# Statistics tiles of the closing rows with six entries instead of five, in a one-core encoder layer

## The chip, the cores and the metric

The kernel runs on one core of a Trainium2 chip. The core has five engines that run beside each other: TensorE (PE, matrix products; its loads of the stationary operand have rows of their own, PEld), VectorE (DVE), ScalarE (ACT), GpSimd (POOL) and SyncE (SP, which issues most of the transfers here). Sixteen transfer engines (DMA) move data between the device memory and the on-chip memory SBUF. SBUF has 128 partitions; a tile takes the same byte range in each of them, so "a tile begins at byte 38,784" means that byte of every partition. Products are summed up in PSUM, a second on-chip memory.

The metric is the device time of one launch in microseconds. The median of three runs is given, and beside it the time of the execution that was profiled.

## What is computed

One layer of an encoder for 256 positions and width 2,048, in float32: windowed attention with rotary positions and a sink, a squared-ReLU MLP with 8,192 hidden values, both with a scale, shift and gate that are worked out from a condition vector `c`, and a LayerNorm behind each.

```python
mod = c_act @ mod_w[i] + mod_b[i]
sh_m, sc_m, g_m, sh_f, sc_f, g_f = jnp.split(mod, 6, axis=-1)
hmix = x * (1.0 + sc_m[:, None, :]) + sh_m[:, None, :]
y = windowed_gqa_sink(hmix, positions, ...)
x = layer_norm(DEEPNORM_ALPHA * x + (1.0 + g_m[:, None, :]) * y, ln_mix_g[i], ln_mix_b[i])
hff = x * (1.0 + sc_f[:, None, :]) + sh_f[:, None, :]
y = sq_relu_mlp(hff, mlp_w1[i], mlp_b1[i], mlp_w2[i], mlp_b2[i])
x = layer_norm(DEEPNORM_ALPHA * x + (1.0 + g_f[:, None, :]) * y, ln_mlp_g[i], ln_mlp_b[i])
```

The last line is the one that the edited lines belong to: the closing LayerNorm, whose mean and variance are gathered in the statistics tiles.

## The kernel before

**Weights.** All weights are read once, in pieces of 1 MB: 128 partitions with 8 KB each, one row of 8 KB for each partition. `Stream.loads` (line 228) issues them on SyncE's queue, in the order of a list that is put together ahead of the loop, each as soon as one of the buffers named `raw` is free. Every product of the layer is made in three parts, from operands that are split into a rounded high half and a remainder: ScalarE rounds a half of a `raw` tile into a `wh` tile (line 298), VectorE subtracts it from the `raw` tile into a `wl` tile (line 249), and TensorE multiplies high by high, high by low and low by high. These three are lines 554, 555 and 556 (helper `mm3`), 1112 and 1114 in the MLP's first product, and 1082, 1085 and 1086 in its first block. For the condition's product, `raw` tiles are used as they are, by TensorE (line 362) or by VectorE (line 402).

**Stages.** First come the condition's columns and the query, key and value product, then attention and its output product, then the MLP in four blocks of 2,048 hidden values. In blocks 1 to 3, `ff_mixed` makes a part of the second product with seven instead of eight products of half size (Strassen's scheme): its left operands are tiles `u` (from the pool of tiles named `g4`, which the profile calls `g`) and their sums and differences in a tile `sc` (helper `sides`, lines 1054 to 1059). Its right operands lie in `wh`, `wl` and, for two of four, in a further `raw` tile. Of the seven products four take `sc` as the stationary operand and three take `u`.

**The closing rows.** Behind block 3, `add_gated` (lines 837, 838, 840) multiplies a piece of 128 x 512 by the gate, adds it to the residual and notes its statistics with `bn_stats`: six numbers for a piece, in `st[t]` for row tile t (0 or 1). Row tile 0 has four pieces. Row tile 1 has five, since its last piece is split in two. `norm_scalars` and `last_scalars` then aggregate the numbers (lines 844 and 1267), and the rows are scaled and stored to `out` with rows of 2 KB. There are two pairs of tiles called `st0` and `st1`: one for the LayerNorm behind attention (line 964, four entries) and one for the closing one (line 1247). They share their slots, two for each name, and a slot is as large as the larger of its tiles, rounded up to 32 bytes.

**Where tiles lie.** The pools are laid out one behind the other: constants (`cst`), small tiles (`sml`: `sc`, `mrow`, the attention's scalars, `st0` and `st1`, four tiles of 2 KB that many names share, and the LayerNorm's scalars), then `raw`, `wh`, `wl` and the twenty 4 KB tiles `g4`; last a stretch that holds three more `raw` tiles first and six 4 KB tiles `g4b` later. In the built program of before they begin at these bytes:

| tiles | first begins at | past a multiple of 2,048 |
| --- | --- | --- |
| `sc` (4 KB) | 20,480 | 0 |
| `mrow` (2 x 2 KB) | 24,576 | 0 |
| four shared tiles of 2 KB | 29,824 | 1,152 |
| `raw` (5 x 8 KB) | 38,784 | 1,920 |
| `wh` (5 x 4 KB) | 79,744 | 1,920 |
| `wl` (5 x 4 KB) | 100,224 | 1,920 |
| `g4` (20 x 4 KB) | 120,704 | 1,920 |
| `raw` (3 more), `g4b` (6 x 4 KB) | 202,624 | 1,920 |

The order of the instructions on each engine is set by a scheduler from the order of the code and from priorities (`AHEAD`), partly by hand (`STEPS`, `LOADS`); neither sees an address.

Of the kernel before, what the change touches and what calls it, by code (L numbers as in the profile page):

```python
# [11 lines left out]
F32 = mybir.dt.float32  # L12
# [9 lines left out]
NT = S // 128  # L22
# [38 lines left out]
def hybrid_kernel(ctx: ExitStack, tc: tile.TileContext, a, out: bass.AP):  # L61
    nc = tc.nc
    cst = ctx.enter_context(tc.tile_pool(name="cst", bufs=1))
    sml = ctx.enter_context(tc.tile_pool(name="sml", bufs=4))
# [485 lines left out]
    def part(tiles, t, c):  # L550
        return tiles[c][:, t * 512:t * 512 + 512]
# [282 lines left out]
    def add_gated(ps, t, c, gt, stats, cols=slice(0, 512), n=0):  # L834
        tmp = sml.tile([128, 512], F32, name="tmp", tag="t2", bufs=4)
        z = part(xs, t, c)[:, cols]
        nc.vector.tensor_tensor(tmp[:, cols], ps[:, cols], gt(c)[:, cols], op=OP.mult)
        nc.vector.tensor_add(z, z, tmp[:, cols])
        if stats:
            nc.vector.bn_stats(stats[t][:, c + n], z)  # L840

    def norm_scalars(st):
        mv = sml.tile([128, 2], F32, name="mv")
        nc.vector.bn_aggr(mv, st)
        ve = sml.tile([128, 1], F32, name="ve")
        nc.vector.tensor_scalar_add(ve, mv[:, 1:2], LN_EPS)
        sd = sml.tile([128, 1], F32, name="sd")
        nc.scalar.activation(sd, ve, AF.Sqrt)
        r0 = sml.tile([128, 1], F32, name="r0")
        nc.vector.reciprocal(r0, sd)  # L850
        q = sml.tile([128, 1], F32, name="qq")
        nc.vector.scalar_tensor_tensor(q, r0, ve, r0, op0=OP.mult, op1=OP.mult)
        nc.vector.tensor_scalar(q, q, -0.5, 1.5, op0=OP.mult, op1=OP.add)
        nc.vector.tensor_mul(r0, r0, q)
        return mv, r0
# [67 lines left out]
    for n in range(21):  # L923
# [37 lines left out]
        if n == 16:  # L961
            warm = sml.tile([128, 1], F32, name="warm")
            nc.scalar.activation(warm, eps, AF.Sqrt)
            st = [sml.tile([128, 4, 6], F32, name=f"st{t}", bufs=2) for t in range(NT)]
# [197 lines left out]
    def gather(pm):  # L1162

        y = [part(ys, t, c) for t in range(NT) for c in range(2)]
        w = sml.tile([128, 512], F32, name="w", tag="t2", bufs=4)

        def add(d, *ops):
            return lambda: nc.vector.tensor_add(d, *ops)

        return [add(y[0], y[0], pm[2]), lambda: nc.scalar.copy(w, pm[6]), add(y[1], y[1], pm[3]),  # L1170
                add(y[2], y[2], pm[4]), add(y[0], y[0], pm[1]), add(w, w, pm[1]), add(y[1], y[1], w),
                add(y[1], y[1], pm[5]), add(y[3], y[3], pm[5]), add(w, w, pm[7]), add(y[2], y[2], w),
                add(y[3], y[3], w)]
# [70 lines left out]
    for n in range(2):  # L1244
        for h in range(2):
            nc.gpsimd.dma_start(gb[n][h], a["lnrow"][2 + n:3 + n, h * 1024:h * 1024 + 1024].partition_broadcast(128))
    st = [sml.tile([128, 5, 6], F32, name=f"st{t}", bufs=2) for t in range(NT)]
    mid = gather(pm)
    for f in mid[:2]:
        f()  # L1250
# [13 lines left out]
    def last_scalars(st, g):  # L1264

        mv = sml.tile([128, 2], F32, name="mv")
        keep(nc.vector.bn_aggr(mv, st))
        dm = sml.tile([128, 128], F32, name="dm", tag="t2", bufs=4)
        keep(nc.vector.tensor_scalar(dm, ident, mv[:, 0:1], 0.5, op0=OP.mult, op1=OP.mult))
        sd = sml.tile([128, 1], F32, name="sd")  # L1270
        keep(nc.scalar.activation(sd, mv[:, 1:2], AF.Sqrt, bias=eps))
        ve = sml.tile([128, 1], F32, name="ve")
        keep(nc.vector.tensor_scalar_add(ve, mv[:, 1:2], LN_EPS))
        z = part(xs, 1, 3)
        keep(nc.vector.scalar_tensor_tensor(z, z, mv[:, 0:1], g, op0=OP.subtract, op1=OP.mult))
        r0 = sml.tile([128, 1], F32, name="r0")
        keep(nc.vector.reciprocal(r0, sd))
        q = sml.tile([128, 1], F32, name="qq")
        keep(nc.vector.scalar_tensor_tensor(q, r0, ve, r0, op0=OP.mult, op1=OP.mult))
        keep(nc.vector.scalar_tensor_tensor(q, q, -3.0, r0, op0=OP.add, op1=OP.mult))  # L1280
        return q, dm
# [16 lines left out]
    mv, rstd = norm_scalars(st[0][:, :4])  # L1298
# [7 lines left out]
    gneg = sml.tile([128, 512], F32, name="w", tag="t2", bufs=4)  # L1306
# [21 lines left out]
        keep(nc.tensor.matmul(pw[c], ident, part(xs, 1, c), start=True, stop=False))  # L1328
    with tc.high_priority(200):
        add_gated(pr, 1, 3, g2, st, right, 1)  # L1330
        rstd, dm = last_scalars(st[1], gneg)
    for c in (3, 1, 2, 0):
        z, (g, b) = part(xs, 1, c), affine(c)
        if c < 3:
# [96 lines left out]
```

## Time and profile before

| what | us |
| --- | --- |
| median of 3 runs | 1073.85 |
| lowest and highest | 1073.42 and 1074.5 |
| profiled execution | 1074.7 |
| its span, first to last instruction | 1072.9 |

How to read the rows that follow. A group's row gives the line, the engine, the operation, what is written and read, the shape, how many there are, and behind the bar the busy time in us and the mean of one in ns; behind the second bar stands the idle time of the engine ahead of them. A row by stretch gives for each engine the busy time and, in brackets, the instructions; then the granted clock of TensorE as a share, the mean busy share of the 16 transfer engines, and what they moved in GB/s. A row of a transfer queue gives packets, megabytes and the time that its packets took as a share of 16 engines over the stretch that was asked for. The chain is followed back from the last instruction, at each step to what released it.

The granted clock was 0.999 over the span. The loads of the activations, which are used for comparison below, are these (size of one, and us from issue to landing):

```profile
g<-in_xT SPq DMA_DIRECT2D x2, 512.0 KB, 11.2
...
out<-g SPq DMA_DIRECT2D x4, 256.0 KB, 2.4
out<-g ACTq DMA_DIRECT2D x4, 256.0 KB, 2.5
g<-in_xT SPq DMA_DIRECT2D x3, 256.0 KB, 13.8
```

### The profile page before, as it was taken

The numbers are of one execution on the slowest core, as the hardware profiler recorded it, in microseconds if no ns is written. First come the engines' busy times: TensorE is split into PE (matmuls) and PEld (weight loads), VectorE is DVE, ScalarE is ACT, GpSimd is POOL, SyncE is SP. The second block draws the span as 40 slices with busy tenths as digits, with TensorE's granted clock in tenths as the row PEclk, the third lists the DMA queues.
The fourth block names the chain that finished last, engine by engine and source line by source line (L and its number), as shares of the span: only waits on it lengthen the run. The fifth ranks groups of instructions, "written<-read, shape, count | busy, mean of one in ns | idle before, by whom it ended". The sixth has DMA issues, their size and how long they took to land.

```text
span 1072.9 us, 16023 instructions
## 1 busy us (share of the span) xinstructions
PE 1055.0 (98%) x6188; PEld 856.2 (80%) x6188; DVE 939.5 (88%) x1401; ACT 619.9 (58%) x977; POOL 27.5 (3%) x54
## 2 busy tenths in 40 slices
PE   8999999999999999999999999999999999999998
PEld 6677677667677799988888888788888888888886
DVE  4689999989899998987579899899889887999998
ACT  5433347777672637643367777347677546777740
POOL 1000000001000000000000000000000001000000
PEclk9999999999999999999999999999999999999999
DMA  9999998798965898698725645973554773465742
GB/s 379 419 419 419 421 421 312 278 385 337 379 262 205 333 359 301 263 330 326 284 84 192 235 168 179 375 298 134 219 220 153 289 287 127 181 235 188 257 184 78
DMA packets 43516, 292.72 MB, mean 273 GB/s; under 512 B 5152, under 2 KB 5280, under 8 KB 9648
## 3 DMA queue, kind: packets, MB, share of 16 engines
q1 hardware_dynamic: 39456, 279.85, 67.6%
q0 software_dynamic: 3232, 10.50, 2.9%
q10 hardware_dynamic: 752, 1.35, 0.4%
q8 instruction: 48, 0.79, 0.3%
q14 instruction: 28, 0.23, 0.1%
HBM read 289.57 MB, written 2.11 MB: 272 GB/s over the span
## 4 chain that ended last, share of the span: by engine, by line
PE 83%; DMA 8%; DVE 7%; ACT 1%; issue 1%; SPq 0%; DVEq 0%; ACTq 0%
PE pa L1112 16%; PE pa L554 13%; PE pa L556 13%; PE pa L555 13%; PE pa L1114 8%; DMA raw<-in_modm 4%; PE pa L1085 3%; PE pm L362 3%; PE pa L1086 3%; PE pa L1082 3%; DMA raw<-in_w 2%; DVE g L402 2%; DVE wl L249 1%; PE pa L767 1%; DMA raw<-in_wqkv 1%; DMA raw<-in_modf 1%
## 5 line engine op out<-in xcount | busy, mean ns | idle before, releaser
L298 ACT CAST wh<-raw 128x1024 fp32r<-128x1024 f32 (+1 forms) x332 | 336.2, 1021 | 277.5 <-PE pa L556 150.7
L249 DVE TENSOR_TENSOR wl<-raw,wh 128x1024 fp32r<-128x1024 f32 (+1 forms) x332 | 388.0, 1182 | 68.0 <-ACT wh L298 63.1
L554 PE MATMUL pa<-wh,g 128*128 128x512 f32 x648 | 258.3, 399 | 3.2 <-ACT g L577 2.5
L556 PE MATMUL pa<-wh,g 128*128 128x512 f32 x648 | 253.1, 392 | 2.2 <-DVE g L579 2.2
L555 PE MATMUL pa<-wl,g 128*128 128x512 f32 x648 | 253.3, 391 | 0.8 <-DVE wl L249 0.8
L1112 PE MATMUL pa<-g,wh 128*128 128x512 f32 x768 | 192.3, 392 | 0.0
L1112 PEld LDWEIGHTS pa<-g,wh 128*128 128x128 f32 x768 | 140.6, 188 | 29.1 <-issue 0.8
L554 PEld LDWEIGHTS pa<-wh,g 128*128 128x128 f32 x648 | 121.6, 188 | 40.9 <-issue 6.8
L556 PEld LDWEIGHTS pa<-wh,g 128*128 128x128 f32 x648 | 121.5, 188 | 31.1 <-DVE g L579 4.1
L555 PEld LDWEIGHTS pa<-wl,g 128*128 128x128 f32 x648 | 121.8, 188 | 25.8 <-DVE wl L249 1.3
L1114 PEld LDWEIGHTS pa<-g,wl 128*128 128x128 f32 x768 | 104.7, 190 | 7.6
L1114 PE MATMUL pa<-g,wl 128*128 128x256 f32 x768 | 107.0, 282 | 0.0
L402 DVE SCALAR_TENSOR_TENSOR g<-raw,cact,g 128x1024 f32<-128x1024 f32 x66 | 83.9, 1279 | 4.1 <-DMA raw<-in_modf 2.7
L1085 PE MATMUL pa<-g,wh 128*128 128x256 f32 x256 | 72.9, 285 | 0.3 <-DVE g L1008 0.2
L1082 PE MATMUL pa<-g,wh 128*128 128x256 f32 x256 | 72.7, 285 | 0.3 <-ACT g L1000 0.3
L1086 PE MATMUL pa<-g,wl 128*128 128x256 f32 x256 | 72.3, 283 | 0.0
L249 DVE TENSOR_TENSOR raw<-raw 128x1024 fp32r<-128x1024 f32 x48 | 58.4, 1221 | 0.6 <-ACT raw L298 0.6
L298 ACT CAST raw<-raw 128x1024 fp32r<-128x1024 f32 x48 | 49.8, 1043 | 2.9 <-DVE raw L260 1.6
L1085 PEld LDWEIGHTS pa<-g,wh 128*128 128x128 f32 x256 | 49.1, 192 | 1.4 <-DVE g L1008 0.9
L1082 PEld LDWEIGHTS pa<-g,wh 128*128 128x128 f32 x256 | 49.0, 192 | 0.8 <-ACT g L1000 0.8
L1086 PEld LDWEIGHTS pa<-g,wl 128*128 128x128 f32 x256 | 49.1, 192 | 0.0
L402 DVE SCALAR_TENSOR_TENSOR g4b<-raw,cact,g4b 128x1024 f32<-128x1024 f32 x32 | 40.1, 1280 | 10.1 <-DMA raw<-in_modgf 10.1
(234 smaller groups left out, 1256.1 us busy)
## 6 DMA issues: line engine op xcount, KB each, us to landing
raw<-in_w1b SPq DMA_DIRECT2D x48, 1024.0 KB, 6.5
raw<-in_w SPq DMA_DIRECT2D x40, 1024.0 KB, 7.2
raw<-in_modm SPq DMA_DIRECT2D x32, 1024.0 KB, 12.3
raw<-in_modf SPq DMA_DIRECT2D x32, 1024.0 KB, 7.3
raw<-in_wqkv SPq DMA_DIRECT2D x24, 1024.0 KB, 13.0
raw<-in_w2s SPq DMA_DIRECT2D x24, 1024.0 KB, 4.9
raw<-in_modgm SPq DMA_DIRECT2D x16, 1024.0 KB, 6.5
raw<-in_wo SPq DMA_DIRECT2D x16, 1024.0 KB, 7.0
```

Source lines behind the costliest of these rows:

```text
L249: self.pinned(nc.vector.tensor_sub(l[:, :w], r, f32(self.hs[n])[:, :w]))
L298: self.pinned(nc.scalar.copy(h[:, :s.shape[-1]], s))
L362: i = nc.tensor.matmul(self.ps[32 * j:32 * j + 32, :w], lhsT[j] if type(lhsT) is list else lhsT, rhs[j], start=self.first, stop=stop)
L402: nc.vector.scalar_tensor_tensor(p[:, :e], s, cact[:, kt:kt + 1], p[:, :e], op0=OP.mult, op1=OP.add)
L554: nc.tensor.matmul(ps, xh, wh, start=start, stop=False)
L555: nc.tensor.matmul(ps, xh, wl, start=False, stop=False)
L556: S.prev = nc.tensor.matmul(ps, xl, wh, start=False, stop=stop).ins
L1082: x = nc.tensor.matmul(o, wh(w, 128), hh, start=new, stop=False)
L1085: nc.tensor.matmul(o, wh(w, 128), hl, start=False, stop=False)
L1086: nc.tensor.matmul(o, wl(w, 128), hh, start=False, stop=end)
L1112: nc.tensor.matmul(ps, wh(k, 128), ff_in(k), start=k == 0, stop=False)
L1114: nc.tensor.matmul(ps[:, :256], wl(k, 128), ff_in(k)[:, :256], start=False, stop=k == NK - 1)
```

## The change

The closing statistics tiles get room for six entries instead of five. The one aggregate that took the whole tile takes its first five entries.

```diff
-    st = [sml.tile([128, 5, 6], F32, name=f"st{t}", bufs=2) for t in range(NT)]
+    st = [sml.tile([128, 6, 6], F32, name=f"st{t}", bufs=2) for t in range(NT)]
...
-        rstd, dm = last_scalars(st[1], gneg)
+        rstd, dm = last_scalars(st[1][:, :5], gneg)
```

A tile of before has 5 x 6 x 4 = 120 bytes for each partition and a slot of 128; now it has 144 bytes and a slot of 160. With four slots, all that lies behind them is moved by 4 x 32 = 128 bytes:

| tiles | begin at, before | now | past a multiple of 2,048, now |
| --- | --- | --- | --- |
| `sc`, `mrow` | 20,480; 24,576 | the same | 0 |
| four shared tiles of 2 KB | 29,824 | 29,952 | 1,280 |
| `raw` | 38,784 | 38,912 | 0 |
| `wh` | 79,744 | 79,872 | 0 |
| `wl` | 100,224 | 100,352 | 0 |
| `g4` | 120,704 | 120,832 | 0 |
| `raw` (3 more), `g4b` | 202,624 | 202,752 | 0 |

The instructions of all engines stand in the same order as before, with the same operands by name, the same buffers and the same waits.

## The prediction

> **What bounds the kernel now.** I read the page first: shares, then the 40 slices, then the chain that ended last.
>
> ```profile
> span 1072.9 us, 16023 instructions
> ...
> PE 1055.0 (98%) x6188; PEld 856.2 (80%) x6188; DVE 939.5 (88%) x1401; ACT 619.9 (58%) x977; POOL 27.5 (3%) x54
> ...
> GB/s 379 419 419 419 421 421 312 278 385 337 379 262 205 333 359 301 263 330 326 284 84 192 235 168 179 375 298 134 219 220 153 289 287 127 181 235 188 257 184 78
> ...
> PE 83%; DMA 8%; DVE 7%; ACT 1%; issue 1%; SPq 0%; DVEq 0%; ACTq 0%
> ```
>
> TensorE is busy 98% of the span and carries 83% of the chain; transfers carry 8%, which is 86 us. The rate row shows that the transfers are not spread evenly: from the second slice to the sixth it stands still at 419 to 421 GB/s, and it never does so again. So there are two regimes, and I asked for busy time by stretch around their border, and for the chain of the first 170 us.
>
> ```profile
> core 0: us, PE busy (x) PEld busy (x) DVE busy (x) ACT busy (x) POOL busy (x), PEclk, DMA share, GB/s
> 27.00:134.00 107.00, 101.05 (x892) 74.59 (x891) 88.33 (x130) 36.87 (x50) 1.91 (x2) 1.00 1.01 419
> 134.00:161.00 27.00, 27.00 (x132) 19.59 (x131) 25.80 (x35) 12.17 (x16) 0.00 (x0) 1.00 1.01 420
> ```
>
> Up to 134 us the 16 transfer engines are full (share 1.01) while TensorE has 107 - 101.05 = 5.95 us of idle time: the loads set the pace there, and what they gain TensorE can use, up to 5.95 us. From 134 to 161 us it has none, though the engines are still full: it works off what has come, and a lead gained by 134 us is kept. Later, transfers matter only where the chain names them.
>
> ```profile
> by line: DMA raw<-in_modm 24.3%; PE pa L554 15.4%; PE pa L556 15.0%; PE pa L555 14.4%; PE pm L362 10.6%; DMA raw<-in_wqkv 6.6%; DVE g L402 2.2%; issue 1.9%; PE pa L177 1.6%; PE pt L745 1.0%; SPq L228 1.0%; PE pa L664 0.8%; PE pa L767 0.7%;
> ...
> 2.58 11.97 DMA raw<-in_modm
> ```
>
> Of the chain's 86 us of transfers, (24.3% + 6.6%) x 170 = 53 us lie in these first 170 us, and 33 us are scattered behind them. The loads begin at 2.6 us, so the stretch that they pace is 134 - 2.6 = 131 us long.
>
> **The change part by part.** No instruction is added, removed or moved on any engine, and no wait changes. Only addresses do: four small tiles take 32 bytes more each, so everything that is allocated behind them begins 128 bytes later. That includes every buffer that a load fills, and nearly every operand. Before, those tiles begin 1,920 bytes past a multiple of 2,048 (so half-way between two multiples of 256), afterwards on one. The distances between them stay as they are. So the sum has no term for a step of the program; it has a term for each way in which an address could set a duration.
>
> The statistics themselves: the same 9 writes of 6 numbers each go into rows of 36 numbers instead of 30, and the two aggregates still read 24 and 30 numbers that lie side by side. I take 0 for these.
>
> *Term 1, loads into the moved buffers.* Every load of before writes SBUF at such a half-way address, so the trace holds no load on the other kind. It is bounded by what a row pays beyond its bytes. A saturated 8 KB row takes 1.01 x 16 engines x 8,192 B / 419 GB/s = 316 ns. For 2 KB rows I use a stretch in which the loads of xT pass, then the closing stores, which read such addresses and write `out`.
>
> ```profile
> DMA packets 111, 0.30 MB, mean 396 GB/s; under 512 B 14, under 2 KB 14, under 8 KB 95
> ...
> q1 hardware_dynamic: 111, 0.30, 100.7%
> ```
>
> ```profile
> DMA packets 304, 0.56 MB, mean 371 GB/s; under 512 B 32, under 2 KB 32, under 8 KB 304
> ...
> q10 hardware_dynamic: 229, 0.44, 78.7%
> q1 hardware_dynamic: 75, 0.12, 22.3%
> ```
>
> The first is 62.00 to 62.75 us: 14 completions, 81 rows of 2 KB and 16 of 8 KB took 1.007 x 16 x 750 = 12,084 ns. Without 16 x 316 and 14 x 9.75 (from the next row) 6,891 ns are left, 85.1 ns a row. The second is 1,061.0 to 1,062.5 us: (1.01 x 16 x 1,500 - 32 x 9.75) / 272 = 88.0 ns a row. A load, which writes off a 256-byte line in SBUF, is not dearer than a store, which does not write there. From 85.1 and 316 ns a byte costs (316 - 85.1) / 6,144 = 0.0376 ns, and what a row pays beyond its bytes is 85.1 - 77.0 = 8.1 ns. The small packets of the gate's row (892 to 895 us) show the same lot where many begin on a line:
>
> ```profile
> DMA packets 129, 0.02 MB, mean 8 GB/s; under 512 B 128, under 2 KB 128, under 8 KB 128
> ...
> q0 software_dynamic: 128, 0.01, 2.6%
> ...
> row<-mrow POOLq DMA_DIRECT2D x8, 2.0 KB, 4.4
> ```
>
> Four rows of 2 KB went as 128 packets, half of them pieces of 128 bytes one behind the other, half completions; every other piece begins off a 256-byte line. They took 0.026 x 16 x 3,000 / 128 = 9.75 ns on average, of which 64 x 0.0376 = 2.4 ns for the average 64 bytes and 7.3 ns fixed. If a start off the line costs x and the rest is a base b, large rows say b + x = 8.1 and these say b + x / 4 = 7.3, so x = 1.1 ns. That is within what rounding of the shares allows (half a unit of 1.01 alone moves 8.1 by about 0.9), so I take x = 0 and keep 1.1 as the end: 1.1 / 316 = 0.34% of 131 + 33 us, a gain of 0.6 us at most. A loss I exclude: any unit up to 2 KB that a transfer is cut into fits the new start at least as well. Its cover would be none: the stretch is paced by these rows.
>
> The Trainium skill, page "DMA: Bandwidth & Descriptors", section "How a descriptor splits into AXI transactions", speaks for more: by it a descriptor that does not start on a 256-byte boundary is cut from the boundary below, and the unused bytes cost beats as well. By it x would be the time of 128 bytes; no row here shows a write to SBUF that starts on the boundary, and the small packets speak against it, as the first rival works out.
>
> *Term 2, engines that read or write the moved tiles.* `sc` is one large tile that stands on a multiple of 2,048 before and after. It serves as the stationary operand of some products whose neighbours take theirs from `u`, a moved tile; the moving rows come from the same `raw` and `wh` buffers. Per form, groups of the whole run (line, operation, tiles, count, busy us, mean ns):
>
> ```profile
> L554 PE MATMUL pm<-raw,sc 128*128 128x512 f32 x24 | 9.5, 395 | 0.0
> L555 PE MATMUL pm<-raw,sc 128*128 128x512 f32 x24 | 9.6, 400 | 0.0
> L556 PE MATMUL pm<-raw,sc 128*128 128x512 f32 x24 | 9.6, 400 | 0.0
> L554 PE MATMUL pt<-raw,sc 128*128 128x512 f32 x24 | 9.4, 394 | 0.0
> L555 PE MATMUL pt<-raw,sc 128*128 128x512 f32 x24 | 9.4, 391 | 0.0
> L556 PE MATMUL pt<-raw,sc 128*128 128x512 f32 x24 | 9.5, 394 | 0.0
> L554 PE MATMUL pa<-raw,g 128*128 128x512 f32 x24 | 9.5, 396 | 0.0
> L555 PE MATMUL pa<-raw,g 128*128 128x512 f32 x24 | 9.3, 388 | 0.0
> L556 PE MATMUL pa<-raw,g 128*128 128x512 f32 x24 | 9.4, 392 | 0.0
> ```
>
> With `sc` the means are 398.3 and 393.0 ns, with `u` (the `g` rows) 392.0: 1.0 to 6.3 ns more, and not the same in two groups with the same tiles, so it goes by the place in the sequence and not by the address. There are 4 products x 3 matmuls x 24 = 288 with `sc`, so the ends are 288 x 6.3 = 1.8 us either way; I take 0. VectorE shows the same:
>
> ```profile
> L1059 DVE TENSOR_TENSOR sc<-sf,sc 128x512 fp32r<-128x512 f32 x24 | 16.4, 684 | 0.0
> L1031 DVE TENSOR_TENSOR g<-uf,g 128x512 fp32r<-128x512 f32 x8 | 5.5, 682 | 0.0
> ```
>
> A subtraction that reads and writes `sc` takes 684 ns, the same one on a moved tile 682. A change of 2 ns would be 0.3%, and VectorE has idle time, so again 0.
>
> Sum: 1,074.7 us (the profiled execution: span 1,072.9 and 1.8 around it) + 0 + 0. That execution lies 0.85 us over the median of the three runs, which is what the forecast is for: **1,073.8 us**, the median rounded.
>
> **The rivals.**
>
> *Loads get cheaper.* If a row that starts half-way between lines pays for the half that it doesn't use, x is 128 x 0.0376 = 4.8 ns, 1.5% of a row. Over 131 + 33 us that is 2.5 us, and TensorE's 5.95 idle us can take the first part: 1,071.4 us, 0.23% faster. It is what the rule of the Trainium skill's page named above would do here. For it: 8.1 ns beyond the bytes has room for 4.8. Against it: b would be 3.3 ns, and the small packets would average 3.3 + 1.2 + 2.4 = 6.9 ns where 9.75 were measured. Chance 0.10.
>
> *`sc` counts after all.* It now has the same offset to the moving rows as `u` has; 1.8 us less, 1,072.0 us, which is still within 0.2%. Against it the two unequal groups. Chance 0.04.
>
> *Loads and streams meet.* With 2 KB rows on 2 KB lines, a transfer's row and the row that TensorE streams can lie in one 2 KB block whole. If SBUF served such blocks one at a time, a matmul would stall. The row with the price is the matmul in the saturated stretch, 30 to 160 us (shortest, median and longest ns):
>
> ```profile
> L554 PE MATMUL pa<-wh,g x135: 387/389/501, 30.5 to 159.7; 128*128 128x512 f32 x135
> ```
>
> The longest is 501 - 389 = 112 ns over the median. Lines 554 to 556 have about 3 x 135 = 405 such matmuls there; if one in ten met it, 40 x 0.112 = 4.5 us, 1,078.3 us. It decides from one in nineteen on (2.15 us is 0.2%, or 19 stalls). Against it: under the full load the median is 2 ns above the shortest, and matmuls whose moving rows already lie inside one block are no slower than those that cross into the next:
>
> ```profile
> L1085 PE MATMUL pa<-g,wh 128*128 128x256 f32 x256 | 72.9, 285 | 0.3 <-DVE g L1008 0.2
> L1082 PE MATMUL pa<-g,wh 128*128 128x256 f32 x256 | 72.7, 285 | 0.3 <-ACT g L1000 0.3
> ```
>
> L1082 streams the first half of a 4 KB tile's 2 KB piece, from byte 1,920 of a block across its end, L1085 the second half, from byte 896 to 1,920 inside it: 285 ns both. Chance 0.07.
>
> *The change doesn't do what it says* is closed: in the built program `raw`, `wh`, `wl` and both kinds of 4 KB tile begin on multiples of 2,048.
>
> **How the numbers follow.** Forecast 0.79, and the three rivals 0.10, 0.04 and 0.07. A measurement of this kernel can tell about 0.2%, 2.15 us, from no change. Faster is most of the first rival, 0.09; slower is the third, 0.07; the rest, 0.84, is within. The range adds the unknowns to 1,073.8: below, 0.6 + 1.8 = 2.4 us, which also takes in the first rival's 1,071.4, so 1,071.3; above, 1.8 us, so 1,075.6. Left out are the third rival and a rest of the others, about 1 in 10.
>
> **What would show it right or wrong.** Right: the stretch 27 to 134 us again at a share of 1.01 and 419 to 420 GB/s, with about 5.95 us of TensorE idle time; 8 KB rows at 316 ns; 388 to 400 ns for the matmuls on `sc` and `u` shown; 682 and 684 ns for the two subtractions. The first rival would show at once as 425 GB/s there and an earlier end of the full share. The second shows in the `sc` rows alone, the third in a median or many single matmuls above 389 ns before 160 us. If the time moved by over 2 us with all these unchanged, an address effect that no row of before hints at would be at work.

## The result, and the profile after

| what | before | changed |
| --- | --- | --- |
| median of 7 runs, us | 1074.50 | 1070.82 |
| lowest and highest, us | 1073.42 to 1075.56 | 1069.94 to 1072.27 |
| profiled execution, us | 1074.7 | 1070.19 |
| its span, us | 1072.9 | 1068.4 |

The ratio is 0.9966, with a 95% interval of 0.9955 to 0.9978: 3.7 us faster. The forecast was no change, 1,073.8 us, in a range from 1,071.3 that the median lies below. It had given faster a chance of 0.09 and no change one of 0.84.

The page of the changed kernel (its span, busy times, rate in 40 slices, shares of the chain):

```profile
span 1068.4 us, 16023 instructions
...
PE 1052.7 (99%) x6188; PEld 856.0 (80%) x6188; DVE 939.2 (88%) x1401; ACT 619.7 (58%) x977; POOL 27.5 (3%) x54
...
GB/s 383 425 424 426 426 427 289 285 380 347 381 261 198 347 358 295 259 327 307 311 81 196 236 168 178 382 295 130 225 223 157 285 286 128 183 236 193 257 181 79
...
PE 86%; DMA 7%; DVE 5%; ACT 1%; issue 1%; SPq 0%; DVEq 0%; ACTq 0%
```

The instructions are as many as before. The plateau from the second slice to the sixth has gone from 419 to 421 GB/s up to 424 to 427, and the share of transfers in the chain from 8% to 7%. By stretch:

```profile
27.00:134.00 107.00, 102.90 (x899) 75.84 (x898) 90.05 (x132) 38.29 (x51) 1.91 (x2) 1.00 1.01 425
134.00:161.00 27.00, 27.00 (x133) 19.61 (x132) 25.80 (x35) 11.48 (x15) 0.00 (x0) 1.00 1.01 424
```

The transfer engines are as full as they were (1.01), and move 425 instead of 419 GB/s. An 8 KB row takes 1.01 x 16 x 8,192 / 425 = 311.5 ns where it took 316. TensorE's idle time in this stretch falls from 5.95 to 4.10 us, so 1.85 us are gained there. (These are single executions. In those of the experiments below it is 4.10 to 4.38 us at 425 GB/s, leaving out the run whose matmuls are dearer there, and 5.59 to 5.95 us at 419 GB/s, so the gain is 1.2 to 1.85 us.)

The trace also holds the time of every single row that was moved, and there the change is plainer than in the sums. Before, 33% of the 8 KB rows that started in this stretch took 309 ns or less, and 66% took 310 to 326. In the changed kernel 99.6% took 309 ns or less. The means are 314.6 and 309.9 ns (316 and 311.5 above come from rounded shares). So a start off the line isn't a charge on each row: a third of the rows went without it.

The loads are half of the gain. The other half lies after 540 us, where blocks 1 to 3 of the MLP mix the seven products with the next hidden values. The groups that the prediction quoted with `sc` as the stationary operand, in the changed kernel:

```profile
L555 PE MATMUL pm<-raw,sc 128*128 128x512 f32 x24 | 9.4, 390 | 0.0
L554 PE MATMUL pm<-raw,sc 128*128 128x512 f32 x24 | 9.3, 390 | 0.0
L556 PE MATMUL pm<-raw,sc 128*128 128x512 f32 x24 | 9.3, 390 | 0.0
```

In the order of these rows, they took 400, 395 and 400 ns and now take 390, all three alike. Not every group with `sc` went there: of the twelve, `pa<-wh,sc` of line 556 takes 408 ns now and took 409, and `pa<-raw,sc` of line 555 took 393 and takes 395, though everything agrees now. Counts times means of the twelve add up to 114.2 us before and 113.0 now, 1.3 us less. (A recorded time is longer than the distance to the next matmul: where 389 ns are recorded, the next one starts after 227 ns.) What the change is worth as a whole shows in line 1112, whose matmuls run from the beginning to the end of such a block. For the third block the trace of before and that of the changed kernel say (shortest, median and longest ns, then when the first and the last begin):

```profile
L1112 PE MATMUL pa<-g,wh x256: 387/389/499, 890.3 to 1009.5; 128*128 128x512 f32 x128
```

```profile
L1112 PE MATMUL pa<-g,wh x256: 389/389/499, 886.5 to 1005.0; 128*128 128x512 f32 x128
```

119.2 us before, 118.5 now: 0.7 us gained by the block itself. The first block gains 0.7 us in the same way (543.1 to 662.2 us before, 541.1 to 659.5 now) and the second 0.6 us (717.0 to 836.0, 713.8 to 832.2), 2.0 us in the three. That is more than the 1.3 us of the products with `sc`. The rest lies in the matmuls around them, whose own operands begin at the same place in both kernels: the busy time of line 1112 fell by 1.0 us, from 192.3 to 191.3. Together with the 1.85 us of the loading stretch that is 3.85 us, near the 3.7 us by which the medians differ. The two profiled spans differ by 4.5 us. Most of what is left was gained between the end of the first block and the start of the second, 54.3 us instead of 54.8. That stretch took from 54.3 to 55.3 us in the executions of the experiments, on both sides of 54.8, so its half microsecond is not put down to the change.

### The profile page after: what moved, and what is told of

The parts are those of the page before. It is cut to its first block, busy times and chain, and to the rows that moved or that the text cites. A ratio compares the mean times of both kernels' runs of the same rounds, so it can differ in the third digit from the quotient of the medians.

```text
span 1068.4 us, 16023 instructions
## 1 busy us (share of the span) xinstructions
PE 1052.7 (99%) x6188; PEld 856.0 (80%) x6188; DVE 939.2 (88%) x1401; ACT 619.7 (58%) x977; POOL 27.5 (3%) x54
## 4 chain that ended last, share of the span: by engine, by line
PE 86%; DMA 7%; DVE 5%; ACT 1%; issue 1%; SPq 0%; DVEq 0%; ACTq 0%
PE pa L1112 16%; PE pa L554 14%; PE pa L556 13%; PE pa L555 13%; PE pa L1114 9%; DMA raw<-in_modm 4%; PE pm L362 3%; PE pa L1085 3%; PE pa L1086 3%; PE pa L1082 3%; PE pa L767 1%; DVE g L402 1%; PE pt L811 1%; PE pa L828 1%; DMA raw<-in_w 1%; DMA raw<-in_wqkv 1%
## 5 line engine op out<-in xcount | busy, mean ns | idle before, releaser
L1112 PE MATMUL pa<-g,wh 128*128 128x512 f32 x768 | 191.3, 391 | 0.0
```

The costliest lines, as they stand in the source:

```text
L1112: nc.tensor.matmul(ps, wh(k, 128), ff_in(k), start=k == 0, stop=False)
```

## The experiments

Two theories were tested against rivals. A tile is "on a line" here when it begins at a multiple of 256 bytes. **Loads:** in a stretch in which transfers are full, a row that starts off a line in SBUF costs more. **Phase:** a matmul costs more when its stationary tile and its moving tile begin at different places within 256 bytes; before, that was so for `sc` alone among the large tiles. All kernels leave the order of the instructions as it was and only leave bytes free between tiles. `gap` tiles are never used. Each ratio is to runs of the kernel before on the same chip.

### Only the large tiles moved

```diff
-    raws = ctx.enter_context(tc.tile_pool(name="raws", bufs=RAWS))
+    ctx.enter_context(tc.tile_pool(name="gap1", bufs=1)).tile([128, 32], F32, name="gap1"); raws = ctx.enter_context(tc.tile_pool(name="raws", bufs=RAWS))
```

> Edit: the statistics tiles stay at five entries; instead 128 bytes are left free in front of the first raw tile, so raw, wh, wl and the 4 KB tiles begin on multiples of 2,048 and everything in front of them, the four shared 2 KB tiles too, stays where it was before. Theory A (two effects: loads into buffers that begin on a 256-byte line, and stationary tiles sc that begin at the same offset within 256 bytes as the moving rows): all of the gain, ratio to before 0.996 to 0.998, 425 GB/s in 27 to 134 us, 390 ns for the three matmuls pm<-raw,sc. Rival (the shared 2 KB tiles or the statistics tiles matter): part of the gain is missing, ratio 0.998 or above.

Ratio 0.9965 (0.9951 to 0.9978), median 1,071.35 us. The stretch row has 425 GB/s and 102.85 us of TensorE; `pm<-raw,sc` takes 390 ns three times:

```profile
27.00:134.00 107.00, 102.85 (x900) 75.81 (x898) 89.92 (x132) 38.28 (x51) 1.91 (x2) 1.00 1.01 425
```

So the statistics tiles and the shared 2 KB tiles have no part in it that shows. Room for a sixth entry is only a way to push what lies behind.

### `sc` moved along: loads alone

```diff
-    fixed = sml.tile([128, 1024], F32, name="sc", bufs=1)
+    cst.tile([128, 32], F32, name="gap0"); fixed = sml.tile([128, 1024], F32, name="sc", bufs=1)
```

> Edit: before with 128 bytes left free in front of sc, so sc, mrow and all behind them move by 128: the large tiles begin on multiples of 2,048 as in the changed kernel, but sc begins 128 bytes past one. Theory A: the loads' part alone, 425 GB/s in 27 to 134 us and about 1.8 us less; the matmuls pm<-raw,sc stay at about 398 ns and the 2.5 us of the mixed blocks are not gained; ratio about 0.9983. Rival (the moving rows on a boundary are what counts, wherever sc is): both parts, 390 ns, ratio about 0.996.

Ratio 0.9982 (0.9973 to 0.9991), 1,073.35 us. By stretch, by group, and for line 1112 in the third block:

```profile
27.00:134.00 107.00, 102.64 (x898) 75.72 (x897) 89.78 (x132) 38.10 (x51) 1.91 (x2) 1.00 1.01 425
```

```profile
L555 PE MATMUL pm<-raw,sc 128*128 128x512 f32 x24 | 9.6, 400 | 0.0
L556 PE MATMUL pm<-raw,sc 128*128 128x512 f32 x24 | 9.6, 399 | 0.0
L554 PE MATMUL pm<-raw,sc 128*128 128x512 f32 x24 | 9.5, 395 | 0.0
```

```profile
L1112 PE MATMUL pa<-g,wh x256: 387/390/499, 887.9 to 1007.0; 128*128 128x512 f32 x128
```

The loads' half is there (425 GB/s, 4.36 us idle instead of 5.95). The matmuls are back at 398 ns on average, and the block at 119.1 us, although all moving rows begin on a line now. The rival, by which the boundary of the moving rows counts, falls.

### All tiles off the line by the same: phase alone

The changed kernel with the `gap0` of the run above.

> Edit: the changed kernel with 128 bytes left free in front of sc: sc and all large tiles begin 128 bytes past a multiple of 2,048, so all share an offset, but none is on a 256-byte line. Theory A: the mixed blocks' part alone: 390 ns for pm<-raw,sc, 419 GB/s in 27 to 134 us, ratio about 0.9977. Rival (the boundary counts, for both): 398 ns, 419 GB/s, ratio 1.000.

Ratio 0.9988 (0.9980 to 0.9997), 1,073.59 us.

```profile
27.00:134.00 107.00, 101.41 (x894) 74.88 (x893) 88.81 (x131) 37.11 (x50) 1.91 (x2) 1.00 1.01 419
```

```profile
L1112 PE MATMUL pa<-g,wh x256: 388/389/499, 890.4 to 1008.9; 128*128 128x512 f32 x128
```

Here the loads are at 419 GB/s as before, `pm<-raw,sc` takes 390 ns three times, and the third block 118.5 us. Neither `sc` nor a large tile is on a line, so it is the difference between the tiles that counts. The ratio is weaker than the 0.9977 that was expected. In the profiled execution the second block lasted 119.2 us, with 1.0 us in which a weight load waited for ScalarE; whether the other ten runs lost that too isn't shown. The two halves alone, 0.0018 and 0.0012, make 0.0030 of the 0.0034, within their intervals.

### The `g4` tiles set apart

```diff
-    gen = ctx.enter_context(tc.tile_pool(name="gen", bufs=20))
-    rows = ctx.enter_context(tc.tile_pool(name="rows", bufs=2, space=bass.MemoryType.DRAM))
+    ctx.enter_context(tc.tile_pool(name="gap4", bufs=1)).tile([128, 32], F32, name="gap4"); gen = ctx.enter_context(tc.tile_pool(name="gen", bufs=20))
+    ctx.enter_context(tc.tile_pool(name="gap5", bufs=1)).tile([128, 32], F32, name="gap5"); rows = ctx.enter_context(tc.tile_pool(name="rows", bufs=2, space=bass.MemoryType.DRAM))
```

> Edit: the changed kernel with 128 bytes left free in front of the twenty 4 KB tiles g4 and 128 behind them: raw, wh and wl stay on multiples of 2,048, and the g4 tiles, which hold the stationary operands of most products (and the moving ones of the MLP's first product), begin 128 bytes past one. Theory A: the products of g4 with wh and wl now take what sc took before, some 5 to 10 ns more each; with about 3,500 of them on TensorE's path 10 to 30 us more, ratio 1.01 to 1.03; 425 GB/s where transfers are full. Rival (the boundary of the moving row counts, or sc is a case of its own): little change against the changed kernel, ratio 0.995 to 0.999.

Ratio 1.0047 (1.0035 to 1.0060), 1,079.84 us: slower than the kernel before, and 8.5 us slower than the run with only the large tiles moved, on the same chip. From 500 to 530 us, where TensorE never idles, this kernel first, then the changed one:

```profile
L554 PE MATMUL pa<-wh,g x44: 390/393/404, 500.0 to 530.0; 128*128 128x512 f32 x44
```

```profile
L554 PE MATMUL pa<-wh,g x44: 389/389/389, 500.3 to 529.5; 128*128 128x512 f32 x44
```

The sign and the price of one are as the phase theory has them: 390 to 404 ns instead of 389 throughout. The starts in these rows (43 steps of three matmuls each) give 233 ns of TensorE's time for a matmul instead of 226. The sum is below the 10 to 30 us expected. Part of it falls where TensorE has idle time to take it up (up to 134 us that falls from 4.10 to 3.40 us), and not every shape pays: line 1086, with 256 columns, has a median of 281 ns instead of 283.

### How fine the line is: 256, 192 and 64 bytes, and `sc` at 64

Three kernels change only the size of `gap1`: 256 bytes on the changed kernel, 64 and 192 on the one before. A fourth has 64 bytes of `gap0` and 64 of `gap1` on the one before.

> Edit: the changed kernel with 256 bytes left free in front of the first raw tile: all large tiles begin 256 bytes past a multiple of 2,048, sc stays on one. Theory (the unit is 256 bytes or less, for both effects): as the changed kernel, 425 GB/s in 27 to 134 us, 390 ns for pm<-raw,sc, ratio to before 0.995 to 0.998. Rival (multiples of 2,048 count): 419 GB/s and 398 ns, ratio 1.000; or one of the two, ratio about 0.998.

> Edit: before with 64 bytes left free in front of the first raw tile, so the large tiles begin 192 bytes past a 256-byte line (1,984 past a multiple of 2,048), sc on one. Loads, three theories: a row pays for the bytes between the line and its start (192 x 0.0376 = 7.2 ns on 311.5, so 415 GB/s); any start off the line costs the same as at 128 (419); the unit is 64 bytes or less (425). Matmuls on sc (now 64 bytes from the moving rows' place within 256): about 398 ns if any difference counts, 390 if only one of 128 does. Ratio 0.996 to 1.002.

> Edit: before with 192 bytes left free in front of the first raw tile, so the large tiles begin 64 bytes past a 256-byte line, sc on one. Loads: by bytes between line and start 64 x 0.0376 = 2.4 ns, 422 GB/s; any start off the line 419; a unit of 64 or less 425. Matmuls on sc: about 398 ns if any difference within 256 counts, 390 if only one of 128 does. Ratio 0.996 to 1.000.

> Edit: before with 64 bytes left free in front of sc and 64 in front of the first raw tile: the large tiles begin on multiples of 2,048, sc 64 bytes past one. Loads 425 GB/s by every theory. Matmuls on sc: 398 ns and ratio about 0.998 if any difference within 256 bytes counts (and then the same as in the run with the large tiles 192 past a line, which has the same difference of 64), 390 ns and ratio about 0.9966 if only 128 does; in between if the price grows with the difference.

| large tiles past a 256-byte line | `sc` minus moving tile, within 256 | ratio to before | GB/s, 27 to 134 us | `pm<-raw,sc`, mean ns |
| --- | --- | --- | --- | --- |
| 0 (256 past 2,048) | 0 | 0.9971 (0.9960 to 0.9982) | 425 | 390.0 |
| 192 | 64 | 1.0003 (0.9993 to 1.0012) | 419 | 395.7 |
| 64 | 192 | 0.9985 (0.9976 to 0.9994) | 419 | 392.0 |
| 0 | 64 | 0.9983 (0.9973 to 0.9992) | 425 | 395.7 |

The means are over three groups each. Those of the second and the fourth kernel, in this order:

```profile
L554 PE MATMUL pm<-raw,sc 128*128 128x512 f32 x24 | 9.5, 397 | 0.0
L556 PE MATMUL pm<-raw,sc 128*128 128x512 f32 x24 | 9.5, 396 | 0.0
L555 PE MATMUL pm<-raw,sc 128*128 128x512 f32 x24 | 9.5, 394 | 0.0
```

```profile
L554 PE MATMUL pm<-raw,sc 128*128 128x512 f32 x24 | 9.5, 397 | 0.0
L556 PE MATMUL pm<-raw,sc 128*128 128x512 f32 x24 | 9.5, 396 | 0.0
L555 PE MATMUL pm<-raw,sc 128*128 128x512 f32 x24 | 9.5, 394 | 0.0
```

They differ in the addresses of `sc` and of every large tile but not in the difference, and the nanoseconds are the same. For the loads, a line of 256 bytes is enough, a multiple of 2,048 isn't needed, and a start 64, 128 or 192 bytes past it costs the same in sum: 419 GB/s. It is made up differently: at 64 and 192 bytes only 10% and 8% of the rows took 309 ns or less, against 33% at 128, but the dearer ones were less dear (means of all rows 315.1, 315.0 and 314.6 ns).

### Only `raw` on a line

On the kernel before: `gap1` of 128 bytes, 128 more in front of `wh` and 128 behind the `g4` tiles.

> Edit: before with 128 bytes left free in front of the first raw tile, 128 behind the five raw tiles and 128 behind the g4 tiles: the raw tiles (and the late region) begin on a 256-byte line, wh, wl and g4 stay 128 bytes past one, sc on one. Theory (the loads' gain hangs on the raw tiles alone; products cost by the difference of stationary and moving tile): 425 GB/s in 27 to 134 us and 1.5 to 1.8 us less there; pm<-raw,sc, both on a line now, 390 ns, but pa<-wh,sc stays dear and pa<-raw,g, now 128 apart, gets dearer (390 to 400 ns); sum ratio 0.997 to 0.999. Rival (the casts' or the g4 tiles' place speeds the loading stretch up): 419 GB/s, ratio 1.000.

Ratio 0.9975 (0.9964 to 0.9986), 1,072.90 us.

```profile
27.00:134.00 107.00, 102.73 (x899) 75.92 (x898) 90.10 (x132) 38.30 (x51) 1.91 (x2) 1.00 1.01 425
```

The whole gain of the loading stretch is there, with `wh`, `wl` and `g4` 128 bytes past a line: it hangs on the buffers that loads fill. `pa<-raw,g` got dearer as expected, 394.0 ns on average where it was 392.0. But `pm<-raw,sc` fell to 393.7 ns on average and not to 390, though its two operands agree here. So the difference within one matmul is not the whole rule.

The traces show one reason. A stationary tile is loaded while the matmul ahead is still at work. In 18 places the last product with `u` and `wh` (line 556) stands right ahead of the first with `sc`, and the load of `sc` begins 3 to 4 ns after that matmul's start. In the kernel before, in the run with `sc` moved along and in this one, that matmul takes 396 ns (median), though its own tiles agree: the `sc` that is being loaded differs by 128 bytes from its moving tile. With the `g4` tiles set apart it takes 389 ns, though its own tiles differ by 128: the `sc` that is being loaded agrees. There, the tile that is being loaded counts, and a difference of 64 or 192 bytes costs nothing (388 ns). Whether that holds at all other places wasn't settled.

### Constants on a line too

On the changed kernel, `ident`, `onesr`, `onesf` and `cact` are moved to lines.

> Edit: the changed kernel with the constants that TensorE reads (ident, onesr, onesf and the condition's column cact) on 256-byte lines as well; all large tiles and sc on lines too, 256 bytes later. Theory (a product costs by the difference of its two operands): these are operands of transposes and of the condition's products, of 128 columns or fewer rows, about 1,000 in all, so up to 1 us less than the changed kernel, ratio to before 0.995 to 0.997. Rival (only long streams of 512 columns show it): as the changed kernel, 0.9966 within its interval.

Ratio 0.9956 (0.9940 to 0.9973). This is the ratio of four runs. The interval holds 0.9966, so no difference to the changed kernel is shown.

## Why the prediction was wrong, by its steps

**What bounds the kernel** was right. The loads pace TensorE up to 134 us, and what they gained there, 1.85 us, reached the end: the first block of line 1112 starts 2.0 us earlier (541.1 instead of 543.1 us).

**No step of the program is changed** was right; only addresses count.

**Term 1 failed in its size.** The prediction derived an extra of 1.1 ns for a row that starts off the line, called it rounding and took 0. Measured: 316 - 311.5 = 4.5 ns, over the stretch 1.85 us. The failing step is the pair of equations. It compared rows with the small packets of the gate, took the fixed part of both to be the same, and took the extra to be paid by every packet off the line. The small packets went when the engines were nearly idle (2.6% of 16 engines), and what a start off the line costs shows where the engines are full: from 200 to 540 us, at a share of 0.82, 79% of the 8 KB rows of before took 309 ns or less with the same start off the line (86% in the changed kernel). The comparison with the closing stores failed likewise, since it set two uses off the line side by side and no use on it. No load of before started on the line, so the first rival's price, 4.8 ns and 425 GB/s, belonged in the range as its end. That this price came so near is luck in part: it was a price that each row pays, and a third paid none.

**Term 2 failed in its value, and in what it counted.** The bound was 1.8 us either way, for the 288 matmuls with `sc`. These gained 1.3 us, and the blocks 2.0 us, since matmuls beside them got cheaper as well; the term had taken those at nothing. The value 0 rested on two groups with the same tiles and different means, 398.3 and 393.0 ns, from which the prediction concluded that place and not address decides. Both were dear against the 390 of the changed kernel; how much of the price shows differs by place. The rows that were closest to the case, the products with `sc` against those with `u`, had the right sign and were set aside. For VectorE the value 0 was right: the sums of its busy time differ by 0.3 us.

**The rivals.** The first and the second came true together, each in its direction and near its size. The prediction priced them as alternatives, with 2.4 us below its centre, where its own terms, 2.5 us for the loads and 1.8 us for the phase, sum to 4.3 us. Two independent effects of one edit add up, and the range should have held both. The third, loads that meet streams, is shown wrong: from 30 to 160 us the median of line 554 is 389 ns before and in the changed kernel.

**The page's rule.** The Trainium skill, page "DMA: Bandwidth & Descriptors", section "How a descriptor splits into AXI transactions", makes a descriptor that starts off a 256-byte boundary fetch from the boundary below. It speaks of what a transaction reads; the tiles moved here are what a load writes. The runs agree with the boundary of 256 bytes. They come near the price at 128 bytes (an estimate of 4.8 ns, by 128 bytes of a row's rate; 4.5 measured). They differ on how it grows: by the bytes below the start the estimate is 2.4 ns at 64 and 7.2 ns at 192, or 422 and 415 GB/s, and both were 419. And they differ on who pays, since some rows off the line took as little as those on it.

Why the loads' price comes out the same for all three offsets stays open, and so does why a difference between the tiles slows a matmul; the runs show on what they depend, not by what means.

## What to carry to other kernels

Look at where tiles begin before counting instructions: put buffers that loads fill on 256-byte lines, and give the stationary and the moving tiles of long matmuls that follow each other the same place within 256 bytes. A small tile in front of them can undo both. A price that is worked out from transfers on idle engines is no price for full ones, and when no row shows a case, its far end belongs in the range, added to those of other effects that the same edit can have.

## What was not expected of the hardware

- With 512 columns, matmuls whose stationary and moving tiles begin at different places within 256 bytes are up to 10 ns dearer on 390, in the groups `pm<-raw,sc`. The price isn't symmetric: 395.7 ns on average at a difference of 64 bytes, 398.3 at 128, 392.0 at 192.
- A matmul whose own tiles agree took 396 ns instead of 389 while a stationary tile 128 bytes apart was being loaded for the next one.
- In the stretch with full engines, a start off a 256-byte line costs 4.5 ns of a row's 316 on average, at 64, 128 and 192 bytes alike, and at 128 bytes a third of the rows paid nothing.
